# A two-layer sparse-attention and state-space trunk: mask products of four 256-column matmuls, a split PSUM pool, four first tiles side by side, and a bias write in four

## The chip, the cores and the metric

One core of a Trainium2 chip runs the whole program. The metric is the device time of one execution in microseconds (us); lower is better.

## What is computed

The reference is a two-layer trunk on 512 tokens of width 2048, all in float32. Cut to what matters here:

```python
# layer 1: sparse attention, 16 heads of 128; an indexer of 16 small heads picks 128 keys per query
proj = rmsnorm(x) @ w_in                      # q, k, v, gate, index q, index k, index weights
score = einsum('bqsh,bqh->bqs', relu(iq . ik), iw);  idx = top_k(score, 128)
logits = q . k[idx] * scale + rel_bias[rel_bucket(t - idx)]
x = x + (softmax(logits) @ v[idx] * silu(g)) @ w_out
# layer 2: Mamba-2 scan, 64 heads of 64 in 8 groups, chunks of 128 tokens
cb = einsum('bclgn,bcsgn->bgcls', c_, b_)
y_diag = einsum('bgcls,bgrcls,bcsgrp->bclgrp', cb, exp(segsum(a)), x_)   # the masked part
y_off  = einsum('bclgn,bcgrpn,bgrcl->bclgrp', c_, prev_states, exp(a_cs))
x = x + rmsnorm((y_diag + y_off + d_skip * xs) * silu(z), norm_w) @ w_out
```

## The kernel before

**Precision by halves.** A float32 operand is split into a high and a low half, both of a type that TensorE takes in one pass: ScalarE casts the high half (`wh`, `xh`, ...), VectorE subtracts to get the low half (`wl`, `xl`, ...). A product is then three matmuls: high by high, high by low, low by high.

**The dense stream.** Nearly all of TensorE's work is a list of weight tiles (`tiles`), cut into `units` of four blocks of 128 rows. A unit is four steps (a step is a call of `mm`: three matmuls of up to 512 columns into one PSUM bank `acc`). Unit `j` is split into halves while unit `j-3` multiplies (`LEAD`). Each 1 MB tile (`raw`) is loaded by SyncE (SP) when the buffer of the tile three before it is free. The first five tiles are special: for them a unit is four blocks of one tile, and the units go round the five tiles, with loads of 256 KB (`rawu`), first by SP and then by ScalarE's queue.

**The threads.** Everything else (indexer, attention heads, convolution, scan, norms) is written as Python generators that emit instructions between the steps; `yield n` means "go on n steps later". So TensorE's order is fixed when the program is built: small matmuls stand between dense ones, and if an operand is late, TensorE stands still, since it runs in order. The same holds for each other engine.

**The parts that the change touches.**
- `bias_setup` writes a table of relative biases to DRAM (`bias_scr`, 3 MB) by one transfer on SP's queue, during the indexer.
- `index_thread` computes the scores `dots`; `head_thread` computes one attention head: scores `sps`, probabilities in `la`, `lb`, `lc`, their transposes `ptp` in the order of key blocks 0, 1, then 2 and 3, and the products `av` and `av3`.
- `cb_thread` computes C·B for a group, in eight groups: `cpa` holds two products of 256 columns; `cpb` two of 128 columns (blocks 1 and 3), and the transposes of B.
- `m_make` and `m_mul` work for each of 32 pairs of heads: `m_make` builds the masked decay matrices of the blocks 0, 2 (256 columns each) and of the small blocks 1 and 3 together, splits them into `mh` and `ml`, and `m_mul` multiplies them by the scaled inputs `xdhl`, into `y0`, `y1` (256 columns a matmul) and `yc`.
- All PSUM tiles rotate through one pool, `banks`, of eight banks.

Of the kernel before, what the change touches and what calls it, by code (L numbers as in the profile page):

```python
# [42 lines left out]
def kernel(  # L43
# [23 lines left out]
    banks = ctx.enter_context(tc.tile_pool(name="banks", bufs=8, space=bass.MemoryType.PSUM))  # L67
# [9 lines left out]
    def PS(name):  # L77
        return banks.tile([P, S], F32, tag="s", name=name)

# [40 lines left out]
    def cols_load():  # L120
        sy.dma_start(out=cols, in_=cols_in)
        ve.tensor_scalar(out=cols[:, C_CW:C_D], in0=cols[:, C_CW:C_D], scalar1=0.5, scalar2=None, op0=ALU.mult)
# [51 lines left out]
    class Dense:  # L174
        def __init__(self, src, ncol, nk, operand, evac, t0=0, t1=S, packed=False, early=None,
                     order=None, keep=(), given=None):
# [14 lines left out]

        def load_unit(self, u, eng):
            r = T("rawu")
            eng.dma_start(out=r, in_=self.src[:, 4 * u : 4 * u + 4].rearrange("p k j -> p (k j)"))
            self.raw[u] = r
# [18 lines left out]
        def mm(self, u, kk):  # L214
            first = u == self.order[0] and kk == 0
            if first:
                self.acc = PS("acc")
# [19 lines left out]
    class TokenMajor:  # L237
# [21 lines left out]
        def mm(self, u, b):  # L259
            if u == 0 and b == 0:  # L260
                self.acc = [PS("acc") for _ in range(NB)]
# [8 lines left out]
            if u == 15:  # L270
                run(self.evac(out, b))

# [60 lines left out]
    def load_x(k, eng):  # L333
        xf[k] = T("x")
        eng.dma_start(out=xf[k], in_=xT[k])
# [20 lines left out]
    def bias_setup():  # L356
# [10 lines left out]
        sy.dma_start(out=dst, in_=rs[:HA, None, :384].to_broadcast([HA, P, 384]))  # L367
# [38 lines left out]
    def index_thread(iw):  # L406
# [9 lines left out]
        for i in range(1, NB):  # L416
# [91 lines left out]
    def head_thread(h):  # L508
# [43 lines left out]
        for grp in ((0,), (1,), (2, 3)):  # L552
# [182 lines left out]
    def evac_bc(g, which):  # L735
        def go(ps):
# [6 lines left out]
            if which is chl:  # L743
                spawn(cb_thread(g), 11)
        return go

    def cb_thread(g):
        bh, bl, bv = bhl.pop(g)
        ch, cl, _ = chl.pop(g)
        cba, cbb = T("cba"), T("cbb")  # L750
        pa, pb = PS("cpa"), PS("cpb")
        for s, pp in ((0, pa[:, :256]), (2, pa[:, 256:]), (1, pb[:, :P]), (3, pb[:, P:256])):
# [7 lines left out]
        for s in range(2):  # L760
            te.transpose(pb[:, 256 + s * P : 256 + (s + 1) * P], bv[:, s * P : (s + 1) * P], ident)
# [5 lines left out]
        yield 1  # L767
        ve.tensor_tensor(out=cut(cbb)[:, :2], in0=cut(pb)[:, :2], in1=tri2, op=ALU.mult)
        bth, btl = T("bth", F32R)[:, :256], T("btl", F32R)[:, :256]
        yield from split(bth, btl, pb[:, 256:])  # L770
# [45 lines left out]
    def xdt_make(p, d2):  # L816
# [14 lines left out]
        highs, lows = (slice(0, 4, 3), slice(0, 2)), (slice(1, 3), slice(2, 4))  # L831
        for c in range(2):
            sc.copy(out=parts[c][:, :, highs[c]], in_=heads2(v)[:, c:4:2])
        yield HOP
        for c in range(2):
            sub(parts[c][:, :, lows[c]], heads2(v)[:, c:4:2], f(parts[c][:, :, highs[c]]))
        xdt[p] = st

    def pairs_thread(p):
# [6 lines left out]
        yield 8  # L846
# [26 lines left out]
    def m_make(p, m):  # L873
# [19 lines left out]
        hi, lo = T("mh", F32R), T("ml", F32R)  # L893
        yield 1
        yield from split(hi, lo, t)
# [8 lines left out]
    def m_mul(p, m, hi, lo):  # L904
        m_next[0] = (p, m + 1) if m < 2 else (p + 1, 0)
        m_tiles.setdefault(p, []).append((hi, lo))
        if m == 2:
            tiles_m = m_tiles.pop(p)
            ys, yc = [PS("y0"), PS("y1")], PS("yc")
            stat = lambda s, n: xdt[p][s % 2][:, 256 * (s // 2) + P * n : 256 * (s // 2) + P * (n + 1)]  # L910
            two = lambda a: a.rearrange("p (e l) -> p e l", e=2)
            for s, (hi, lo) in zip((0, 2), tiles_m):
                for e in range(2):
                    x = stat(s, e)
                    out = ys[e][:, 128 * s : 128 * s + 256]
                    te.matmul(out, x, hi[:, 256 * e : 256 * e + 256], start=s == 0, stop=False, skip_group_check=True)  # L916
                    te.matmul(out, x, lo[:, 256 * e : 256 * e + 256], start=False, stop=True, skip_group_check=True)  # L917

            hi, lo = tiles_m[2]
            for i, s in enumerate((1, 3)):  # L920
                ls, out = slice(i * P, (i + 1) * P), two(yc[:, 256 * i : 256 * i + 256])
# [11 lines left out]
            odd = lambda a: a.rearrange("p (c h l) -> p c h l", h=2, l=P)  # L933
            for e in range(2):
                r, q = slice(64 * e, 64 * e + 64), slice(64 - 64 * e, 128 - 64 * e)
                ve.scalar_tensor_tensor(out=v[r], in0=x[r], scalar=col(C_D, p)[r], in1=ys[e][r],
                                        op0=ALU.mult, op1=ALU.add)
                yield 1
                add(v[r], v[r], ys[e][q])
                yield 1  # L940
                add(odd(v[r])[:, :, 1], odd(v[r])[:, :, 1], odd(yc[r])[:, :, e])
# [59 lines left out]
    def evac_ob(j):  # L1001
        def go(ps):
            t = PS("x2p") if j >= KD - 5 else T("x2")
# [57 lines left out]
    EARLY_TILES = 5  # L1061
    for t in range(8):
        dense(wa[t], P, 16, opA, evac_iq(t), t0=P, early=t if t < EARLY_TILES else None)
        if t == EARLY_TILES - 1:
            for u in range(4):
                for d in tiles:
                    units.append((d, u))
# [3 lines left out]
    for h in range(HA):  # L1071
# [5 lines left out]
        dense(wa[24 + 2 * h], P, 16, opA, evac_q(h))  # L1077
        dense(wa[25 + 2 * h], P, 16, opA, evac_k(h))
# [28 lines left out]
    at_unit(40, lambda: spawn(bias_setup(), 0))  # L1107
# [175 lines left out]
```

## Time and profile before

| what | value |
|---|---|
| time, median of 3 runs | 2418.91 us (2417.77 to 2419.24) |
| the profiled execution, its own time | 2418.09 us |
| its span, first to last instruction | 2416.4 us |
| TensorE matmuls busy | 2399.8 us, 99% of the span |
| VectorE busy | 1582.5 us, 65% |
| ScalarE busy | 1072.4 us, 44% |
| mean granted TensorE clock | 0.999 of full speed |

The busy time of an engine is the time in which at least one of its instructions was running. Matmuls overlap, so the cost of one in a stream is read from start to start, not from its duration. "Idle before" in brackets is the time for which the engine stood still, with the instruction that ended it.

### The profile page before, as it was taken

What the parts mean: (1) busy time and instruction counts of PE and PEld (TensorE: products, weight loads), DVE (VectorE), ACT (ScalarE), POOL (GpSimd) and SP (SyncE); (2) the same over time, 40 slices, a digit from 0 to 9 for tenths busy, and PEclk for the clock granted to TensorE, in tenths of its full rate; (3) what the DMA queues carried; (4) which work ended last, traced back from release to release, by engine and by line L of the source; (5) the groups of instructions that cost most, each with busy time, mean ns of one, the idle gap of its engine ahead of it and who ended that gap; (6) DMA issues with size and microseconds to landing.
All of it is one profiled execution on the core that took longest, in us unless ns stands there. A gap on an engine that the chain in (4) does not pass through costs nothing.

```text
span 2416.4 us, 29873 instructions
## 1 busy us (share of the span) xinstructions
PE 2399.8 (99%) x11398; PEld 2016.2 (83%) x11398; DVE 1582.5 (65%) x2891; ACT 1072.4 (44%) x2134; POOL 1.2 (0%) x8
## 2 busy tenths in 40 slices
PE   9999999999999999999999999999999999999998
PEld 9878888888888888888888888888888888888887
DVE  6569466464654654358788888888888888433334
ACT  6433233333333433234556565565656566322222
POOL 0000000000000000000000000000000000000000
PEclk9999999999999999999999999999999999999999
DMA  6362322222222224433333333333334344333333
GB/s 223 103 130 88 107 93 74 92 90 90 94 79 93 82 105 142 146 122 130 122 108 119 118 122 126 127 127 106 124 107 142 112 149 157 127 114 100 101 113 109
DMA packets 83440, 278.54 MB, mean 115 GB/s; under 512 B 7744, under 2 KB 40928, under 8 KB 58208
## 3 DMA queue, kind: packets, MB, share of 16 engines
q1 hardware_dynamic: 78976, 266.41, 33.0%
q10 hardware_dynamic: 4320, 10.23, 1.2%
q8 instruction: 89, 1.46, 0.3%
q14 instruction: 55, 0.45, 0.1%
HBM read 258.32 MB, written 18.02 MB: 114 GB/s over the span
## 4 chain that ended last, share of the span: by engine, by line
PE 96%; DVE 2%; DMA 2%; issue 0%; ACT 0%; SPq 0%; DVEq 0%; ACTq 0%
PE acc L229 27%; PE acc L231 27%; PE acc L230 27%; PE acc L265 2%; PE acc L267 2%; PE acc L266 2%; DMA raw<-wa 2%; PE ptp L558 1%; PE y L917 1%; PE y L916 1%; PE xst L819 1%; PE sps L525 0%; PE sps L526 0%; PE sps L524 0%; PE av L588 0%; PE av L586 0%
## 5 line engine op out<-in xcount | busy, mean ns | idle before, releaser
L90 DVE TENSOR_TENSOR wl<-raw,wh 128x512 fp32r<-128x512 f32 (+1 forms) x788 | 528.7, 684 | 136.8 <-ACT wh L206 96.2
L206 ACT CAST wh<-raw 128x512 fp32r<-128x512 f32 (+1 forms) x724 | 427.0, 613 | 173.9 <-PE acc L230 100.1
L229 PE MATMUL acc<-x1h,wh 128*128 128x512 f32 x1280 | 503.4, 393 | 0.0
L230 PE MATMUL acc<-x1l,wh 128*128 128x512 f32 x1280 | 499.5, 390 | 0.0
L231 PE MATMUL acc<-x1h,wl 128*128 128x512 f32 x1280 | 499.2, 390 | 0.0
L229 PE MATMUL acc<-xh,wh 128*128 128x512 f32 (+2 forms) x912 | 353.5, 388 | 2.3 <-ACT wh L206 2.1
L231 PE MATMUL acc<-xh,wl 128*128 128x512 f32 (+2 forms) x912 | 349.6, 383 | 0.3
L230 PE MATMUL acc<-xl,wh 128*128 128x512 f32 (+2 forms) x912 | 348.8, 382 | 0.6 <-DVE xl L101 0.6
L231 PEld LDWEIGHTS acc<-x1h,wl 128*128 128x128 f32 x1280 | 240.4, 188 | 50.9
L229 PEld LDWEIGHTS acc<-x1h,wh 128*128 128x128 f32 x1280 | 240.8, 188 | 46.6
L230 PEld LDWEIGHTS acc<-x1l,wh 128*128 128x128 f32 x1280 | 240.9, 188 | 46.1
L229 PE MATMUL acc<-ygh,wh 128*128 128x512 f32 (+1 forms) x544 | 205.4, 378 | 0.0
L231 PE MATMUL acc<-ygh,wl 128*128 128x512 f32 (+1 forms) x544 | 205.0, 377 | 0.0
L230 PE MATMUL acc<-ygl,wh 128*128 128x512 f32 (+1 forms) x544 | 205.0, 377 | 0.0
L231 PEld LDWEIGHTS acc<-xh,wl 128*128 128x128 f32 (+1 forms) x912 | 170.6, 187 | 35.1 <-DVE wl L90 2.2
L229 PEld LDWEIGHTS acc<-xh,wh 128*128 128x128 f32 (+1 forms) x912 | 170.7, 187 | 31.8 <-ACT wh L206 2.6
L230 PEld LDWEIGHTS acc<-xl,wh 128*128 128x128 f32 (+1 forms) x912 | 171.0, 187 | 29.8 <-DVE xl L101 1.4
L231 PEld LDWEIGHTS acc<-ygh,wl 128*128 128x128 f32 x544 | 102.4, 188 | 18.8
L230 PEld LDWEIGHTS acc<-ygl,wh 128*128 128x128 f32 x544 | 102.4, 188 | 18.7
L229 PEld LDWEIGHTS acc<-ygh,wh 128*128 128x128 f32 x544 | 102.4, 188 | 18.5
L727 DVE SCALAR_TENSOR_TENSOR hh<-rw,cols,hh 128x511 f32<-128x511 f32 x144 | 107.4, 746 | 6.5 <-ACT hh L724 4.0
L887 ACT ACTIVATE bc<-bc,aloc 128x256 f32<-128x256 f32 (+1 forms) x256 | 102.8, 446 | 0.5
(295 smaller groups left out, 3316.1 us busy)
## 6 DMA issues: line engine op xcount, KB each, us to landing
raw<-wb SPq DMA_DIRECT2D x80, 1024.0 KB, 4.9
raw<-wa SPq DMA_DIRECT2D x48, 1024.0 KB, 4.9
raw<-wbo SPq DMA_DIRECT2D x33, 1024.0 KB, 4.8
bc<-r_scr SPq DMA_DIRECT2D x96, 256.0 KB, 6.1
raw<-wav SPq DMA_DIRECT2D x16, 1024.0 KB, 4.9
raw<-wao SPq DMA_DIRECT2D x16, 1024.0 KB, 5.4
yg_scr<-yy SPq DMA_DIRECT2D x24, 256.0 KB, 4.6
ygr<-yg_scr SPq DMA_DIRECT2D x24, 256.0 KB, 5.1
```

What stands on the lines that cost most here:

```text
L90: ve.tensor_tensor(out=out, in0=a, in1=b, op=ALU.subtract)
L206: sc.copy(out=self.w[u][0], in_=self.raw[u].rearrange("p (k j) -> p k j", k=4))
L229: te.matmul(out[:m], w[0], xh[:, ts], start=first, stop=False)
L230: te.matmul(out[:m], w[0], xl[:, ts], start=False, stop=False)
L231: te.matmul(out[:m], w[1], xh[:, ts], start=False, stop=last)
L265: te.matmul(out, xh[:, bs], wh, start=u == 0, stop=False)
L266: te.matmul(out, xh[:, bs], wl, start=False, stop=False)
L267: te.matmul(out, xl[:, bs], wh, start=False, stop=u == 15)
L558: te.transpose(ps[:, n + (i - j) * P : n + (i - j + 1) * P], prob[i][:, j * P : (j + 1) * P], ident)
L727: ve.scalar_tensor_tensor(out=hh[:, d:], in0=rw[:, : S - d], scalar=col(C_CW, 4 * ct + 3 - d), in1=hh[:, d:], op0=ALU.mult, op1=ALU.add)
L819: te.transpose(ps[:, c * P : (c + 1) * P], xs[p][:, c * P : (c + 1) * P], ident)
L887: sc.activation(out=t3[:, e, a:b], in_=t3[:, e, a:b], func=AF.Relu, scale=-1.0, bias=aloc[:, s, 2 * p + e : 2 * p + e + 1])
```

## The change

It does seven things. (1) The small mask blocks 1 and 3 are laid out differently: for each head of the pair and each chunk the high half and the low half of the matrix stand side by side in 256 columns (`m0`, `m1`), so that four matmuls take the place of six, and they add into the same banks as the large blocks; `y` is now two tiles of two banks each, and VectorE adds the parts. (2) Likewise in `cb_thread`: `cc` holds the halves of C side by side, four matmuls take the place of six, VectorE and ScalarE add the two parts (`cbl`), and the transposes of B go into a bank of their own (`bt`), some steps later. (3) The pool of eight banks becomes one of four and, until shortly before layer 2, a second of four (`banks_a`), which then gives way to two pairs of banks (`banks_b`). (4) The first four tiles run side by side: a unit is one block of rows for four tiles, and all their loads are SP's. (5) The bias table is written in four transfers, 24 steps apart. (6) The transposes `ptp` go in the order 2 and 3, then 1, then 0. (7) The state matmuls `st` are two steps later, and a few starting points shift.

```diff
-    banks = ctx.enter_context(tc.tile_pool(name="banks", bufs=8, space=bass.MemoryType.PSUM))
+    banks = ctx.enter_context(tc.tile_pool(name="banks", bufs=4, space=bass.MemoryType.PSUM))
...
+    early_banks.append(early_banks[0].enter_context(
+        tc.tile_pool(name="banks_a", bufs=4, space=bass.MemoryType.PSUM)))
+    def change_banks():
+        early_banks[0].close()
+        late_banks.append(ctx.enter_context(tc.tile_pool(name="banks_b", bufs=2, space=bass.MemoryType.PSUM)))
...
+    class FourTiles:
...
+        def load(self, k):
+            load_x(k)
+            if k < 4:
+                self.raw[k] = T("rawu").rearrange("p (t j) -> p t j", t=4)
+                sy.dma_start(out=self.raw[k], in_=self.src[:4, :, k].rearrange("t p j -> p t j"))
+            elif k % 4 == 0:
+                r = raw_pool.tile([P, 16 * P], F32, tag="raw", name="raw").rearrange("p (t k j) -> p t k j", t=4, k=4)
+                sy.dma_start(out=r, in_=self.src[:4, :, k : k + 4].rearrange("t p k j -> p t k j"))
...
+        def mm(self, k, t):
+            if k == 0 and t == 0:
+                self.acc = [PSA("acc4")[:, : S - self.t0] for _ in range(4)]
+            wh, wl = [a[:, t * P : (t + 1) * P] for a in self.w[k]]
+            xh, xl = [a[:, self.t0 :] for a in xhl[k]]
+            te.matmul(self.acc[t], wh, xh, start=k == 0, stop=False)
+            te.matmul(self.acc[t], wh, xl, start=False, stop=False)
+            te.matmul(self.acc[t], wl, xh, start=False, stop=k == KD - 1)
...
-        sy.dma_start(out=dst, in_=rs[:HA, None, :384].to_broadcast([HA, P, 384]))
+        for g in range(4):
+            hs = slice(4 * g, 4 * g + 4)
+            sy.dma_start(out=dst[hs], in_=rs[hs, None, :384].to_broadcast([4, P, 384]))
+            yield 24
...
-                ps = PS("dots")
+                ps = PS("dots") if h % 3 == 2 else PSA("dots")
...
-        for grp in ((0,), (1,), (2, 3)):
+        for grp in ((2, 3), (1,), (0,)):
...
+            if s % 2:
+                c2 = cc[:, 256 * (s // 2) : 256 * (s // 2) + 256]
+                te.matmul(pp, bh[:, ss], c2, start=s == 1, stop=False, skip_group_check=True)
+                te.matmul(pp[:, :P], bl[:, ss], c2[:, :P], start=False, stop=s == 3, skip_group_check=True)
+                continue
...
+        sc.copy(out=cut(cbl)[:, :2], in_=cut(pb)[:, 1:4:2])
+        yield 2
+        add(cut(cbl)[:, :2], cut(cbl)[:, :2], cut(pb)[:, 0:4:2])
+        ve.tensor_tensor(out=cut(cbb)[:, :2], in0=cut(cbl)[:, :2], in1=tri2, op=ALU.mult)
+        yield 2
+        pt = PS("bt")
+        for s in range(2):
+            te.transpose(pt[:, s * P : (s + 1) * P], bv[:, s * P : (s + 1) * P], ident)
...
-        yield 8
+        yield 10
         st = PS("st")[:, :256]
...
+            hi, lo = T("m0", F32R), T("m1", F32R)
+            cut = lambda a: a.rearrange("p (c x l) -> p c x l", c=2, x=2)
+            src = t.rearrange("p (e c l) -> p e c l", e=2, c=2)
+            for e, a in enumerate((hi, lo)):
+                sc.copy(out=cut(a)[:, :, 0], in_=src[:, e])
+            yield HOP
+            for e, a in enumerate((hi, lo)):
+                sub(cut(a)[:, :, 1], src[:, e], f(cut(a)[:, :, 0]))
...
-                te.matmul(out, stat(s, 0), two(hi)[:, :, ls], start=i == 0, stop=False, skip_group_check=True)
-                te.matmul(out, stat(s, 0), two(lo)[:, :, ls], start=False, stop=False, skip_group_check=True)
-                te.matmul(out, stat(s, 1), two(hi)[:, :, ls], start=False, stop=i == 1, skip_group_check=True)
+            for c in range(2):
+                for e in range(2):
+                    te.matmul(ys[e][:, c, P : 3 * P], stat(2 * c + 1, e), tiles_m[2][e][:, 256 * c : 256 * c + 256],
+                              start=False, stop=True, skip_group_check=True)
...
+    first = FourTiles(wa, [evac_iq(t) for t in range(4)], P)
+    for k in range(KD):
+        units.append((first, k))
+    for t in range(4, 8):
+        dense(wa[t], P, 16, opA, evac_iq(t), t0=P)
...
+        bank = (lambda: PSA("acca")) if h % 4 in (1, 2) else None
+        dense(wa[24 + 2 * h], P, 16, opA, evac_q(h), bank=bank)
+        dense(wa[25 + 2 * h], P, 16, opA, evac_k(h), bank=bank)
...
+    at_unit(u_b - 16, change_banks)
```

Where this moves instructions, first on TensorE, at the end of the mask products of the first pair of heads; before, the last two products of the large blocks are followed by six for the small blocks, into a tile of their own:

```order
L916 MATMUL y1_9855<-mh_9709,xdhl_9566 128x256
L917 MATMUL y1_9855<-ml_9710,xdhl_9566 128x256
L922 MATMUL yc_9856<-mh_9780,xdhl_9567 128x256
L923 MATMUL yc_9856<-ml_9781,xdhl_9567 128x256
L924 MATMUL yc_9856<-mh_9780,xdhl_9567 128x256
L922 MATMUL yc_9856<-mh_9780,xdhl_9567 128x256
L923 MATMUL yc_9856<-ml_9781,xdhl_9567 128x256
L924 MATMUL yc_9856<-mh_9780,xdhl_9567 128x256
L229 MATMUL acc_9794<-x1h_8593,wh_9762 128x512
```

and now by four of the same width, into the tiles of the large blocks:

```order
L1011 MATMUL y_9848<-mh_9703,xdhl_9557 128x256
L1011 MATMUL y_9848<-ml_9704,xdhl_9557 128x256
L1015 MATMUL y_9847<-m0_9781,xdhl_9558 128x256
L1015 MATMUL y_9848<-m1_9782,xdhl_9558 128x256
L1015 MATMUL y_9847<-m0_9781,xdhl_9558 128x256
L1015 MATMUL y_9848<-m1_9782,xdhl_9558 128x256
L244 MATMUL acc_9786<-x1h_8575,wh_9745 128x512
```

The eight products of the large blocks stay; two of 14 matmuls go, for each of 32 pairs. Second, on TensorE in the C·B products of the first group; before, six of 128 columns and then the two transposes of B, between dense matmuls:

```order
L231 MATMUL acc_9330<-x1h_8203,wl_9282 128x512
L755 MATMUL cpb_9363<-bch_9276,bch_9182 128x128
L756 MATMUL cpb_9363<-bcl_9277,bch_9182 128x128
L757 MATMUL cpb_9363<-bch_9276,bcl_9183 128x128
L755 MATMUL cpb_9363<-bch_9276,bch_9182 128x128
L756 MATMUL cpb_9363<-bcl_9277,bch_9182 128x128
L757 MATMUL cpb_9363<-bch_9276,bcl_9183 128x128
L761 MATMUL cpb_9363<-ident_95,bcv_9136 128x128 x2
L229 MATMUL acc_9330<-x1h_8281,wh_9281 128x512
```

and now:

```order
L246 MATMUL acc_9319<-x1h_8419,wl_9290 128x512
L828 MATMUL cpb_9369<-cc_9281,bch_9168 128x256
L829 MATMUL cpb_9369<-cc_9281,bcl_9169 128x128
L828 MATMUL cpb_9369<-cc_9281,bch_9168 128x256
L829 MATMUL cpb_9369<-cc_9281,bcl_9169 128x128
L244 MATMUL acc_9319<-x1h_8497,wh_9289 128x512
```

Six became four, two of them wider; the two transposes stand 18 dense matmuls later, in their own bank. Third, on SP's queue during the indexer, where `bias_scr<-rs` is the bias table's write and `raw<-wa` are weight tiles (in brackets what each waits for: a place among the outstanding transfers, and VectorE's last read of the buffer); before:

```order
L187 DMA raw<-wa 128x2048 [waits DMAHW3_49,DVE_49]
L367 DMA bias_scr<-rs 2048x1x384 [waits DVE_49]
L187 DMA raw<-wa 128x2048 [waits DMAHW4_49,DVE_49]
L187 DMA raw<-wa 128x2048 [waits DMAHW5_49,DVE_49]
L187 DMA raw<-wa 128x2048 [waits DMAHW6_49,DMAHW2_49,DVE_49]
```

and now:

```order
L432 DMA bias_scr<-rs 512x1x384 [waits DVE_49]
L207 DMA raw<-wa 128x2048 [waits DMAHW7_49,DVE_49]
L207 DMA raw<-wa 128x2048 [waits DMAHW0_49,DVE_49]
L432 DMA bias_scr<-rs 512x1x384 [waits DMAHW1_49]
L207 DMA raw<-wa 128x2048 [waits DMAHW3_49,DMAHW2_49,DVE_49]
L432 DMA bias_scr<-rs 512x1x384
L207 DMA raw<-wa 128x2048 [waits DMAHW7_49,DMAHW4_49,DVE_49]
```

The one write of 3 MB ahead of three loads became pieces of a quarter with weight loads between them; a fourth piece follows two loads later.

## Rows read from the trace of the kernel before

**Rows 1.** Page, part 1: busy us (share of the span) xinstructions.

```profile
PE 2399.8 (99%) x11398; PEld 2016.2 (83%) x11398; DVE 1582.5 (65%) x2891; ACT 1072.4 (44%) x2134; POOL 1.2 (0%) x8
```

**Rows 2.** Waits of PE: engine line <- releaser: us in total, times, longest.

```profile
PE acc L229 <- ACT wh L206: 2.1, 2, 1.7
PE st L852 <- DVE xd2l L90: 1.1, 1, 1.1
PE ptp L558 <- DVE lb L548: 1.1, 1, 1.1
...
PE acc L230 <- DVE xl L101: 0.6, 2, 0.3
```

**Rows 3.** Timeline of PE in one pair's mask products: start us, us, instruction.

```profile
1158.99 0.28 PE L916 MATMUL y<-mh,xdhl 128*128 128x256 f32 x1
...
1159.94 0.28 PE L922 MATMUL yc<-mh,xdhl 128*128 128x256 f32 x1
...
1160.66 0.40 PE L229 MATMUL acc<-x1h,wh 128*128 128x512 f32 x1
```

**Rows 4.** Timeline of PE in the first group's narrow C·B products.

```profile
1107.25 0.22 PE L755 MATMUL cpb<-bch 128*128 128x128 f32 x1
...
1107.86 0.41 PE L761 MATMUL cpb<-ident,bcv 128*128 128x128 f32 x2
```

**Rows 5.** Timeline of PE at a 256-column matmul followed by one of 128.

```profile
374.44 0.28 PE L580 MATMUL av<-pth,vh 128*128 128x256 f32 x1
374.55 0.22 PE L581 MATMUL av<-pth,vl 128*128 128x128 f32 x1
374.61 0.45 PE L229 MATMUL acc<-xh,wh 128*128 128x512 f32 x1
374.89 0.39 PE L230 MATMUL acc<-xl,wh 128*128 128x512 f32 x1
```

**Rows 6.** Timeline of the start; the last two rows are matmuls 13 and 22.

```profile
1.73 0.43 SPq L194 DMA_DIRECT2D rawu<-wa  x1
...
5.65 0.62 ACT L206 CAST wh<-rawu 128x512 fp32r<-128x512 f32 x1 [0.56 <-DMA rawu<-wa]
...
6.32 0.44 PE L229 MATMUL acc<-xh,wh 128*128 128x384 f32 x1 [0.42 <-ACT wh L206]
...
7.05 0.44 PE L231 MATMUL acc<-xh,wl 128*128 128x384 f32 x1
...
10.64 0.34 PE L229 MATMUL acc<-xh,wh 128*128 128x384 f32 x1
...
12.20 0.33 PE L229 MATMUL acc<-xh,wh 128*128 128x384 f32 x1
```

**Rows 7.** Windows: us, busy by engine (x instructions), PEclk, DMA share, GB/s.

```profile
28.00:32.00 4.00, 4.00 (x24) 3.89 (x23) 2.48 (x5) 3.09 (x6) 0.00 (x0) 1.00 1.04 397
116.00:138.00 22.00, 22.00 (x106) 18.41 (x105) 9.78 (x19) 7.65 (x17) 0.00 (x0) 1.00 0.92 100
1360.00:1470.00 110.00, 110.00 (x538) 92.81 (x537) 92.95 (x158) 65.65 (x135) 0.00 (x0) 1.00 0.35 122
```

**Rows 8.** Timeline around the bias write, on SP, ACT and PE.

```profile
113.64 0.66 SPq L367 DMA_DIRECT2D bias_scr<-rs  x1
...
151.41 0.62 ACT L206 CAST wh<-raw 128x512 fp32r<-128x512 f32 x1 [12.23 <-DMA raw<-wa]
...
152.08 0.51 PE L229 MATMUL acc<-xh,wh 128*128 128x512 f32 x1 [1.67 <-ACT wh L206]
```

**Rows 9.** Timeline of PE at the two other waits.

```profile
863.60 0.33 PE L558 MATMUL ptp<-ident,lb 128*128 128x128 f32 x1 [1.06 <-DVE lb L548]
...
1249.95 0.39 PE L852 MATMUL st<-xd2l,bth 128*128 128x256 f32 x1 [1.15 <-DVE xd2l L90]
```

**Rows 10.** Timeline of one attention head, from its last transposes to its product.

```profile
366.61 0.38 PE L558 MATMUL ptp<-ident,la 128*128 128x128 f32 x2
367.03 0.48 ACT L567 CAST pth<-ptp 128x384 fp32r<-128x384 f32 x1 [0.97 <-PE ptp L558]
...
367.88 0.28 DVE L90 TENSOR_TENSOR pth<-ptp,pth 128x128 fp32r<-128x128 f32 x1
...
372.86 0.39 PE L586 MATMUL av<-pth,vh 128*128 128x512 f32 x1
```

**Rows 11.** By tile: op xcount, duration ns min/median/max, first and last start, forms.

```profile
L90 DVE TENSOR_TENSOR btl<-cpb,bth x8: 393/418/421, 1114.5 to 1890.1; 128x256 fp32r<-128x256 f32 x8
...
L90 DVE TENSOR_TENSOR ml<-bc,mh x96: 678/685/695, 1137.8 to 2005.4; 128x512 fp32r<-128x512 f32 x96
```

More of the change, by code (lines that the diff above doesn't have):

```diff
@@ L175, in __init__ @@
         def __init__(self, src, ncol, nk, operand, evac, t0=0, t1=S, packed=False, early=None,
-                     order=None, keep=(), given=None):
+                     order=None, keep=(), given=None, bank=None):
+            self.bank = bank
             self.order = list(order or range(nk // 4))
@@ L216, in mm @@
             if first:
-                self.acc = PS("acc")
+                self.acc = self.bank() if self.bank else PS("acc")
             ts, m = slice(self.t0, self.t1), self.ncol
@@ L260, in mm @@
             if u == 0 and b == 0:
-                self.acc = [PS("acc") for _ in range(NB)]
+                self.acc = [PSA("vacc") for _ in range(NB)]
             wh, wl = self.w[u]
@@ L271, in mm, with __init__, split_hi, split_lo @@
                 run(self.evac(out, b))
+    class FourTiles:
+        given, early, nk = None, True, 64
+        def __init__(self, src, evacs, t0):
+            self.src, self.evacs, self.t0 = src, evacs, t0
+            self.raw, self.w = {}, {}
+        def load(self, k):
[6 more added lines that the diff above has]
+                sy.dma_start(out=r, in_=self.src[:4, :, k : k + 4].rearrange("t p k j -> p t k j"))
+                for i in range(4):
+                    self.raw[k + i] = r[:, :, i]
+        def split_hi(self, k):
+            self.x = prep_x(k)
+            next(self.x)
+            self.w[k] = [T("wh", F32R), T("wl", F32R)]
+            sc.copy(out=self.cut(self.w[k][0]), in_=self.raw[k])
+        def split_lo(self, k):
+            for _ in self.x:
+                pass
+            hi, lo = self.w[k]
+            sub(self.cut(lo), self.raw.pop(k), f(self.cut(hi)))
+        def cut(self, w):
+            return w.rearrange("p (t j) -> p t j", t=4)
+        def mm(self, k, t):
[6 more added lines that the diff above has]
+            te.matmul(self.acc[t], wl, xh, start=False, stop=k == KD - 1)
+            if t == 3:
+                del self.w[k]
+            if k == KD - 1:
+                run(self.evacs[t](self.acc[t]))
     tiles = []
@@ L331, with load_x @@
     xf, xhl = {}, {}
-    def load_x(k, eng):
+    def load_x(k):
         xf[k] = T("x")
-        eng.dma_start(out=xf[k], in_=xT[k])
+        sy.dma_start(out=xf[k], in_=xT[k])
     def prep_x(k):
@@ L743, in go @@
             if which is chl:
+                cc = T("cc", F32R)
+                odd = lambda a: a.rearrange("p (c x l) -> p c x l", c=2, x=2)
+                which[g] = (hi, lo, cc)
+                yield 1
+                yield from split(odd(cc)[:, :, 0], odd(cc)[:, :, 1], odd(v)[:, :, 1])
                 spawn(cb_thread(g), 11)
@@ L892, in m_make @@
         ve.tensor_tensor(out=t3, in0=t3, in1=cb[:, None, :].to_broadcast([P, 2, 256]), op=ALU.mult)
-        hi, lo = T("mh", F32R), T("ml", F32R)
         yield 1
-        yield from split(hi, lo, t)
+        if m < 2:
+            hi, lo = T("mh", F32R), T("ml", F32R)
+            yield from split(hi, lo, t)
+        else:
+            hi, lo = T("m0", F32R), T("m1", F32R)
[6 more added lines that the diff above has]
+                sub(cut(a)[:, :, 1], src[:, e], f(cut(a)[:, :, 0]))
         yield 8
@@ L1059, in mark, with half_of_two @@
         return len(units)
[L1061 to L1067, printed above, removed]
+    both = []
+    def half_of_two():
+        if not both:
+            a = PS2("acc2")
+            both.extend([a[:, 0], a[:, 1]])
+        return both.pop(0)
+    first = FourTiles(wa, [evac_iq(t) for t in range(4)], P)
[3 more added lines that the diff above has]
+        dense(wa[t], P, 16, opA, evac_iq(t), t0=P)
     dense(wai, 80, 16, opA, evac_idx)
@@ L1182, in split_now @@
         d.split_lo(u)
-    x0 = prep_x(0)
-    next(x0)
-    d0, u0 = units[0]
-    d0.split_hi(u0)
-    for _ in x0:
-        pass
-    d0.split_lo(u0)
-    for k in range(1, 4):
-        for _ in prep_x(k):
-            pass
-    for i in range(1, LEAD):
+    for k in range(KD):
+        first.load(k)
+        if k == 11:
+            cols_load()
+    for _ in range(3):
+        load_next()
+    for i in range(LEAD):
         split_now(i)
-    spawn(load_early_thread(), 0)
-    spawn(prep_x_thread(), 3)
-    at_unit(12, cols_load)
+    at_unit(20, scale_cols)
     for i in range(u_end):
```

88 lines of the change are left out of this document (28 added, 60 removed).

## The prediction

> **What bounds the kernel now.** I read the busy times first. TensorE is busy 99% of the span, VectorE 65%, ScalarE 44% [rows 1]: as long as TensorE has its operands, only fewer or cheaper matmuls shorten the program, and work on the other engines is free until something on TensorE waits for it. Next the waits of TensorE, to see how often that is so. Four lines hold what matters: 2.1 us for a weight cast (1.7 of it at one place), and 1.1, 1.1 and 0.6 us at three others [rows 2]. So there are two kinds of gain to look for: matmuls taken out, priced from start to start, and a handful of single waits. The windows then say how much room the other engines have in layer 2, where most of the change lies: VectorE is busy 92.95 of 110 us, ScalarE 65.65 [rows 7].
>
> **1. The mask products.** The 14 matmuls of a pair take from 1158.99 to 1160.66, and the six on `yc` from 1159.94 to 1160.66, 0.72 us, so 0.12 us each [rows 3]. Two of the 14 go, with 32 pairs: 64 x 0.12 = 7.7 us. The other twelve keep their width, so nothing else of this changes on TensorE; I take 7.3 to 7.7 us as bounds, the low one if the first of the new ones, with a new stationary operand each, costs 10 ns more.
>
> On the other engines the pair gets dearer. The one subtraction of 512 columns (0.685 us) becomes two of 256 (0.418 each) [rows 11], 0.15 us more for VectorE, and about as much for ScalarE's cast. With the C·B additions (two more VectorE operations of 256 columns for each group of four pairs, 0.84 us, or 0.21 a pair) it is 0.36 us a pair. The 96 subtractions of 32 pairs lie between 1137.8 and 2005.4 [rows 11], 27 us a pair, so a window of 110 us holds about four pairs, and VectorE would go from 92.95 to about 94.4 of 110 us. That is hidden behind TensorE. The cover would be gone if VectorE had 4 us more work in each pair.
>
> **2. The C·B products.** The six narrow ones take from 1107.25 to 1107.86, 0.61 us [rows 4], 0.10 each though they have half the columns of those at 0.12. So the number of matmuls counts here, and hardly the width. A pair of 256 and then 128 columns is seen elsewhere: it starts at 374.44, the dense matmul after it at 374.61, and the one after that at 374.89, where a dense step costs 0.23; the pair thus costs 374.89 - 374.44 - 0.23 = 0.22 us [rows 5]. Two pairs cost 0.44, a saving of 0.17 us a group, 1.3 us over eight groups. Bounds: 1.0 (0.12 for each of the four) to 2.0 (0.18 a pair, if the small delay behind it is not paid twice). The transposes are only moved.
>
> [...]
>
> **3. The start.** The first real matmul starts at 6.32 and the 13th at 10.64; nine more take until 12.20, 0.173 us each [rows 6]. Twelve at that pace are 2.08 us, so 4.32 - 2.08 = 2.24 us are lost while x blocks land one by one, since the first unit needs four of them. With four tiles side by side, the first unit needs one x block and one weight block. What stays is the wait of the third matmul for the first low half: it starts 0.73 us after the first instead of 0.35, 0.38 us. So up to 1.9 us are to be won. Against it: the first weight block comes in 512-byte pieces, one for each tile and partition, instead of 2 KB ones, and TensorE starts when it is cast (issued at 1.73, cast at 5.65, first matmul at 6.32 [rows 6]). 256 KB at the 397 GB/s of the early window take 0.66 us. How much slower the short pieces are, the trace does not show for loads; the nearest it has is the mix with 1 KB pieces in layer 2, 122 GB/s at a share of 0.35, 349 at a full share, against 397/1.04 = 382 [rows 7]. I take half the speed as an estimate, 0.7 us later, and a gain of 1.2 us. Bounds: 1.9 (no loss), and -3 (a quarter of the speed: 2 us more for each of the first four blocks, of which the x blocks and the split hide about half). After the first four blocks the need is 0.5 MB in 2.08 us, 252 GB/s, against 382: no wait.
>
> [...]
>
> **4. The bias table.** Its write is issued at 113.64, and the DMA engines are then 0.92 busy at only 100 GB/s [rows 7, 8]. A weight tile issued behind it lands so late that ScalarE waits 12.23 us for it, and TensorE 1.67 us for the cast [rows 8]. The 3.1 MB at 100 GB/s are 31 us, and a load that shares the engines with all of that came 1.67 us too late. A quarter takes about 8 us, and the pieces are 24 steps apart, 24 x 3 x 0.23 = 17 us, with weight loads between them, so a load meets one of them at most. The wait should go: 1.7 us, bounds 0 and 2.0 (matmuls right behind a wait are slow too). SP's queue holds nothing urgent besides the weight tiles here.
>
> **5. Two single waits.** `st` moves two steps, six dense matmuls or 1.4 us, later; its wait was 1.15 us [rows 9]: gone, or nearly, 1.1 us (bounds 0.4 and 1.4). What is late next is the state product `yo`, and it moves along with it. The transposes of key blocks 2 and 3 go first now and don't need the last probabilities, written into `lb` just before, which cost 1.06 us [rows 9]; by the time block 0 comes they are there: 1.1 us (bounds 0 and 1.2).
>
> **6. Four banks instead of eight.** A PSUM tile now takes the bank of a tile that was read a short time before. The tightest place in a head is `av`, which follows the last transposes. Their last reader ends at 367.88 + 0.28 = 368.16, and `av` starts at 372.86: 4.7 us of room [rows 10]. The new last group is one of 512 columns; its cast and its subtraction together are about 0.3 us longer, which leaves 4.4. And `av` needs the low half from the same subtraction anyway. Layer 2 has fewer tiles in a given time, and its `y` tiles come back after a whole pair. I take 0, bounds 0 and 3 us: should VectorE run late, a bank wait can cost a few single microseconds, as in rows 2.
>
> **The sum.** 7.7 + 1.3 + 1.2 + 1.7 + 1.1 + 1.1 = 14.1 us. The profiled execution took 2418.09 us, of which its span is 2416.4; 2418.09 - 14.1 = 2404.0. The median of the runs is 0.8 us above the profiled one, so against it the same sum gives 2404.8; I say 2404.3, between the two.
>
> **The rivals.**
> - *Only the matmuls count.* Parts 1 and 2 come, 9 us, but the first blocks land late and the waits only move: the short pieces eat the start's gain, and the indexer, whose VectorE work on the top-k also falls here, still waits once. For it: each of the waits is a single event, which a shift of a few steps could bring back elsewhere. Against it: each has a visible cause that the change removes. 2418.1 - 9 + 0 to 4 = 2409 to 2413.
> - *The four banks make each head wait.* If `av` or the next head's `sps` waited in all 16 heads, it would decide from 14.1/16 = 0.88 us a head; at 2 us a head the sum is 2418.1 - 14.1 + 32 = 2436. For it: banks are halved, and in the heads ten tiles rotate through four. Against it: 4.4 us of room at the tightest place, and VectorE has idle time there.
> - *No change.* The first blocks at a quarter of the speed (-3), bank waits (3 us) and the waits that stay (3.9) take 11 us of 14.1: 2415.
> - *Narrow matmuls cost their columns alone.* Then the C·B part gives nothing, 2418.1 - 12.8 = 2405.3. Rows 4 speak against it. [...]
>
> **How the numbers follow.** The forecast, 11 to 17 us gained, has 0.60, and in it the rule on narrow matmuls 0.04. Only the matmuls: 0.29. No change: 0.06. Slower by the banks: 0.05. Its own range is 2401 to 2407.5. The range for 8 in 10 has to take in the larger part of the second case: 2400.8 to 2411. A measurement can tell 0.2%, 4.8 us, from no change. Faster by more: 0.89; within it: 0.06; slower: 0.05.
>
> **What would show it.** Right: 12 matmuls of 0.12 us for a pair; four in C·B in about 0.45 us; the 13th matmul at 9.5 or so instead of 10.64; no wait of ScalarE for a weight tile near 150 us; in the waits of TensorE none for `wh` of 1.7, none on `st` above 0.5, none on `lb`; TensorE's busy time down by about 9 us. Wrong: a wait of `av`, `sps`, `acc` or `dots` for a reader of an earlier tile, repeated in each head or each group; a first matmul after 8 us; VectorE above 97% in layer 2, with TensorE waiting for `wl`; new matmuls slower than 0.13 us where they write into the second half of a bank already in use.

## The result, and the profile after

The changed kernel takes 2440.1 us (median of four runs, 2439.5 to 2441.6), the kernel before 2418.7: a ratio of 1.009, interval 1.0076 to 1.0105. It is slower by 21 us; forecast were 14 us less.

The page of the profile after, part 1 (busy us by engine), beside [rows 1]:

```profile
PE 2396.7 (98%) x11318; PEld 2011.6 (82%) x11318; DVE 1589.6 (65%) x2939; ACT 1075.6 (44%) x2182; POOL 1.2 (0%) x8
```

Its waits of TensorE (us in total, times, longest), beside [rows 2]:

```profile
PE acc L244 <- ACT wh L221: 31.3, 3, 16.7
```

The only other two lines are 1.1 us at the warm-up and 0.3 us at the end. The waits for `xd2l` and `lb` are gone, as forecast. But the wait for a weight cast, 2.1 us before, is now 31.3 us, in three events. Two of the three on TensorE, and the four waits of ScalarE for weight tiles, by the timelines:

```profile
171.07 0.79 PE L244 MATMUL acc<-xh,wh 128*128 128x512 f32 x1 [8.75 <-ACT wh L221]
202.38 0.80 PE L244 MATMUL acc<-xh,wh 128*128 128x512 f32 x1 [16.72 <-ACT wh L221]
...
135.28 0.62 ACT L221 CAST wh<-raw 128x512 fp32r<-128x512 f32 x1 [9.63 <-DMA raw<-wa]
170.40 0.62 ACT L221 CAST wh<-raw 128x512 fp32r<-128x512 f32 x1 [17.29 <-DMA raw<-wa]
201.71 0.62 ACT L221 CAST wh<-raw 128x512 fp32r<-128x512 f32 x1 [20.59 <-DMA raw<-wa]
235.93 0.62 ACT L221 CAST wh<-raw 128x512 fp32r<-128x512 f32 x1 [15.79 <-DMA raw<-wa]
```

All four lie in the stretch of the bias write. SP's queue there, by the timeline:

```profile
99.31 0.79 SPq L432 DMA_DIRECT2D bias_scr<-rs  x1
100.27 13.02 SPq L207 DMA_DIRECT2D raw<-wa  x2
113.33 3.71 SPq L432 DMA_DIRECT2D bias_scr<-rs  x1
124.98 18.47 SPq L207 DMA_DIRECT2D raw<-wa  x1
143.50 3.87 SPq L432 DMA_DIRECT2D bias_scr<-rs  x1
147.47 31.62 SPq L207 DMA_DIRECT2D raw<-wa  x2
179.14 3.72 SPq L432 DMA_DIRECT2D bias_scr<-rs  x1
```

The weight tiles issued between 99.3 and 133 us, by the view of transfers, with their median time from issue to landing at the end:

```profile
raw<-wa SPq DMA_DIRECT2D x3, 1024.0 KB, 35.0
```

One by one, the six tiles issued from 100 to 183 us took 25 to 54 us; elsewhere a tile takes 5. The windows say why (us, busy by engine, granted clock, mean busy share of the 16 DMA engines, GB/s): the first with the first piece under way, the others around the longest wait.

```profile
101.00:108.00 7.00, 7.00 (x35) 5.88 (x34) 3.44 (x8) 2.54 (x6) 0.00 (x0) 1.00 0.23 25
...
195.00:200.00 5.00, 0.00 (x0) 0.00 (x0) 0.00 (x0) 0.00 (x0) 0.00 (x0) 0.50 0.24 57
200.00:205.00 5.00, 2.62 (x6) 2.09 (x7) 2.64 (x5) 3.29 (x8) 0.00 (x0) 0.50 0.25 89
```

The whole write ran at a share of 0.92 and 100 GB/s [rows 7]; a piece runs at 0.23 and 25 GB/s, a quarter of both. 0.79 MB at 25 GB/s are 31 us, as long as the whole took, and it comes four times: by the packet records the four pieces last 29.5 to 31.5 us from first packet to last, the one write before 31.6. While TensorE stands, its granted clock falls to 0.50; it is still there in the first matmuls afterwards, most of which then take 0.43 us from start to start (172 to 174 us) instead of 0.23. From the first `dots` to the first `sps` the program now takes 345.2 - 99.5 = 245.7 us instead of 311.2 - 100.1 = 211.1: 34.6 us lost, of which 31.3 - 1.7 are waits and some 5 the slow matmuls behind them (they cost 7.0 us now, 1.8 before).

The rest of the change looks as forecast. The timeline after: the start (the first weight cast, then TensorE), the first group's narrow C·B products, and the mask products of one pair, beside [rows 3, 4, 6].

```profile
5.11 0.62 ACT L312 CAST wh<-rawu 128x512 fp32r<-128x512 f32 x1 [0.29 <-DMA rawu<-wa]
...
1.12 6.32 PE L126 MATMUL warm<-ones 128*128 128x128 f32 x28 [1.12 <-DVE ones L123]
7.11 0.50 PE L328 MATMUL acc<-xh,wh 128*128 128x384 f32 x1
...
9.36 0.33 PE L328 MATMUL acc<-xh,wh 128*128 128x384 f32 x1
...
1142.05 0.28 PE L828 MATMUL cpb<-cc,bch 128*128 128x256 f32 x1
...
1142.45 0.46 PE L244 MATMUL acc<-x1h,wh 128*128 128x512 f32 x1
...
1191.95 0.28 PE L1011 MATMUL y<-mh,xdhl 128*128 128x256 f32 x1
...
1192.91 0.64 PE L1015 MATMUL y<-m,xdhl 128*128 128x256 f32 x4
1193.39 0.40 PE L244 MATMUL acc<-x1h,wh 128*128 128x512 f32 x1
```

Matmul 13 starts at 9.36 instead of 10.64; the narrow products take 0.40 instead of 0.61 us; a pair takes 1193.39 - 1191.95 = 1.44 us, twelve times 0.12.

### The profile page after: what moved, and what is told of

Same layout as the page of the kernel before. It is cut to its first block, busy times and chain, and to the rows that moved or that the text cites. A ratio compares the mean times of both kernels' runs of the same rounds, so it can differ in the third digit from the quotient of the medians.

```text
span 2439.5 us, 29717 instructions
## 1 busy us (share of the span) xinstructions
PE 2396.7 (98%) x11318; PEld 2011.6 (82%) x11318; DVE 1589.6 (65%) x2939; ACT 1075.6 (44%) x2182; POOL 1.2 (0%) x8
## 3 DMA queue, kind: packets, MB, share of 16 engines
q8 instruction: 88, 1.44, 0.2%
## 4 chain that ended last, share of the span: by engine, by line
PE 94%; DMA 3%; another core or an unknown queue 1%; DVE 1%; ACT 0%; issue 0%; DVEq 0%; ACTq 0%
PE acc L244 23%; PE acc L245 23%; PE acc L246 23%; DMA raw<-wa 3%; PE acca L244 2%; PE vacc L280 2%; PE acca L246 2%; PE vacc L282 2%; PE acca L245 2%; PE vacc L281 2%; PE y L1011 1%; PE ptp L624 1%; PE y L1015 1%; PE xst L902 1%; PE acc L330 0%
## 5 line engine op out<-in xcount | busy, mean ns | idle before, releaser
L107 DVE TENSOR_TENSOR wl<-raw,wh 128x512 fp32r<-128x512 f32 x804 | 539.6, 684 | 187.6 <-ACT wh L221 143.8
L221 ACT CAST wh<-raw 128x512 fp32r<-128x512 f32 x728 | 429.6, 613 | 225.4 <-PE acc L245 99.9
L244 PE MATMUL acc<-xh,wh 128*128 128x512 f32 (+2 forms) x592 | 232.3, 392 | 31.5 <-ACT wh L221 31.3
L246 PE MATMUL acc<-xh,wl 128*128 128x512 f32 (+2 forms) x592 | 229.1, 387 | 0.0
L245 PE MATMUL acc<-xl,wh 128*128 128x512 f32 (+2 forms) x592 | 229.0, 387 | 0.0
L244 PEld LDWEIGHTS acc<-xh,wh 128*128 128x128 f32 (+1 forms) x592 | 111.8, 189 | 52.5 <-ACT wh L221 33.2
L246 PEld LDWEIGHTS acc<-xh,wl 128*128 128x128 f32 (+1 forms) x592 | 111.4, 188 | 23.4 <-DVE wl L107 1.1
L245 PEld LDWEIGHTS acc<-xl,wh 128*128 128x128 f32 (+1 forms) x592 | 111.9, 189 | 19.4
```

What stands on the lines that cost most here:

```text
L107: ve.tensor_tensor(out=out, in0=a, in1=b, op=ALU.subtract)
L221: sc.copy(out=self.w[u][0], in_=self.raw[u].rearrange("p (k j) -> p k j", k=4))
L244: te.matmul(out[:m], w[0], xh[:, ts], start=first, stop=False)
L245: te.matmul(out[:m], w[0], xl[:, ts], start=False, stop=False)
L246: te.matmul(out[:m], w[1], xh[:, ts], start=False, stop=last)
```

## The experiments

The theory: the pieces of the bias write make the loss, since a transfer from few heads runs on few DMA engines. The rivals: another part does (four banks, the loads of the four tiles); four writes on the queue cost by their number; a tile is late only because it stands behind a piece in the same queue.

**One write again**, the rest as changed.

```diff
-        for g in range(4):
-            hs = slice(4 * g, 4 * g + 4)
-            sy.dma_start(out=dst[hs], in_=rs[hs, None, :384].to_broadcast([4, P, 384]))
-            yield 24
+        sy.dma_start(out=dst, in_=rs[:HA, None, :384].to_broadcast([HA, P, 384]))
```

> The changed kernel with the bias table written by one transfer again. Theory (the four pieces of the bias write make the loss, each taking as long as the whole because four heads use a quarter of the DMA engines): the loss of 34.6 us between the indexer and the first head goes but for the 1.7 us that ScalarE's late weight tile cost before; with 0.6 us from the start, 1.1 us before the last head's transposes and 9.7 us in layer 2, as read in the trace of the change, 2418.7 - 11.4 = 2407.3 us (2405 to 2409). Rival (the waits for weight tiles come from another part: four tiles side by side, whose loads all go by SP's queue, or four banks): the three long waits of TensorE stay and it is above 2430 us.

Measured: 2404.8 us (2403.9 to 2405.2), ratio 0.9941 (0.9929 to 0.9954). The loss of 35.3 us is all this part's. It came out 2.5 us below the working, just under its range, since the working had taken only 0.6 us for the start (below, it is worth 2.2). Its waits of TensorE keep one for a weight cast:

```profile
PE acc L244 <- ACT wh L221: 1.0, 1, 1.0
```

**Only this part in the kernel before**: the same edit the other way round.

> The kernel before with only the bias write in four pieces of four heads, 24 steps apart. Theory: all of the loss shows without any other part of the change: 2418.7 + 34.6 - 1.7 = about 2451 us (2444 to 2456). Rival (the pieces only hurt together with the four first tiles or with four banks): within 3 us of 2418.7.

Measured: 2453.5 us (2453.0 to 2454.6), ratio 1.0143 (1.0130 to 1.0157), 34.8 us slower. No other part is needed. Its line in the waits of TensorE:

```profile
PE acc L229 <- ACT wh L206: 29.2, 3, 16.6
```

**Four pieces by rows of the table**, each with all 16 heads.

```diff
-            hs = slice(4 * g, 4 * g + 4)
-            sy.dma_start(out=dst[hs], in_=rs[hs, None, :384].to_broadcast([4, P, 384]))
+            ps = slice(32 * g, 32 * g + 32)
+            sy.dma_start(out=dst[:, ps], in_=rs[:HA, None, :384].to_broadcast([HA, 32, 384]))
```

> The changed kernel with the bias table still written in four pieces, 24 steps apart, but cut by rows of the table: each piece has 32 of the 128 rows of all 16 heads. Theory (the number of heads in a piece sets how many DMA engines work on it): each piece runs at a share of about 0.92 and 100 GB/s and is done in about 8.4 us, no weight tile lands more than about 12 us after its issue, and the 1.7 us of the one write go too: 2404 to 2407 us. Rival (four writes between the weight loads on one queue cost by their number, or a piece of 768 KB is slow however it is cut): weight tiles still land 30 us or more after their issue, and it is above 2425 us.

Measured: 2402.7 us (2402.6 to 2404.1), ratio 0.9935 (0.9922 to 0.9947). **This version is faster than both kernels.** It lies 1.3 us under the range given, which was built on the same working. So it is not the number of writes nor their size. The view of transfers from 95 to 215 us has the median landing times of weight tiles and pieces:

```profile
raw<-wa SPq DMA_DIRECT2D x8, 1024.0 KB, 5.2
bias_scr<-rs SPq DMA_DIRECT2D x4, 768.0 KB, 9.9
```

All waits of TensorE in it, with none for a weight cast:

```profile
PE warm L126 <- DVE ones L123: 1.1, 1, 1.1
PE bc L1131 <- DVE r L377: 0.3, 1, 0.3
```

**Two pieces of eight heads.**

```diff
-        for g in range(4):
-            hs = slice(4 * g, 4 * g + 4)
-            sy.dma_start(out=dst[hs], in_=rs[hs, None, :384].to_broadcast([4, P, 384]))
+        for g in range(2):
+            hs = slice(8 * g, 8 * g + 8)
+            sy.dma_start(out=dst[hs], in_=rs[hs, None, :384].to_broadcast([8, P, 384]))
```

> The changed kernel with the bias table in two pieces of eight heads, 24 steps apart. Theory (engines by the number of heads): each piece runs at a share of about 0.46 and 50 GB/s and takes about 33 us again, so the engines are held for 66 us instead of 134, and the loss lies between that of one write and of four; with (34.6 - 1.7)/3 = 11 us for each piece after the first, 2407.3 + 11 = about 2418 us (2410 to 2424). Rival (time by bytes): a half takes 17 us at 100 GB/s, and it is at 2405 to 2409 us.

Measured: 2414.3 us (2413.5 to 2415.6), ratio 0.9982 (0.9973 to 0.9991), between one write and four. TensorE's waits hold one line for a weight cast:

```profile
PE acc L244 <- ACT wh L221: 8.5, 2, 8.3
```

The window from 101 to 108 us, of two halves and behind it of one write (the last two columns are share and GB/s), shows the steps: a share of 0.23 with four heads (above), 0.46 with eight, 0.92 with sixteen.

```profile
101.00:108.00 7.00, 7.00 (x35) 5.84 (x35) 3.44 (x8) 2.67 (x6) 0.00 (x0) 1.00 0.46 50
```

```profile
101.00:108.00 7.00, 7.00 (x35) 5.88 (x34) 3.44 (x7) 2.17 (x5) 0.00 (x0) 1.00 0.92 100
```

A share of 0.23 could be four engines at work or sixteen that are slowed. The packets in the trace decide it: in this window the view of transfers counts 114, 230 and 454 of them, which by the shares is 0.23 us of an engine's time for each in all three, and no more than 4, 8 and 16 are ever under way at once. So a piece has fewer engines, and they are not slower.

**The four pieces of heads on ScalarE's queue**: in their line `sc.dma_start` takes the place of `sy.dma_start`.

```diff
-            sy.dma_start(out=dst[hs], in_=rs[hs, None, :384].to_broadcast([4, P, 384]))
+            sc.dma_start(out=dst[hs], in_=rs[hs, None, :384].to_broadcast([4, P, 384]))
```

> The changed kernel with its four pieces of four heads each, but issued on ScalarE's queue, while the weight tiles stay on SP's. First theory (a weight tile is late because a quarter of it stands behind the piece in the same queue on the same four engines): from another queue the tiles pass the pieces and land within about 10 us, TensorE's long waits go, and it is at 2403 to 2408 us. Second theory (the four engines are simply taken, whoever issues): a tile still lands about 35 us after its issue, and it stays near 2440 us. [...]

Measured: 2445.0 us (2444.6 to 2445.1), ratio 1.0107 (1.0092 to 1.0123). The time is near the second theory's, but for a reason that neither named. The landing of the weight tiles, by the view of transfers from 95 to 240 us:

```profile
raw<-wa SPq DMA_DIRECT2D x8, 1024.0 KB, 16.8
```

ScalarE's timeline, with its issues of the third and fourth piece and the operation for which it stood still after the fourth:

```profile
134.18 14.25 ACTq L432 DMA_DIRECT2D bias_scr<-rs  x1
...
160.65 18.98 ACTq L432 DMA_DIRECT2D bias_scr<-rs  x1
...
179.68 0.49 ACT L494 ACTIVATE relu<-dots 128x384 f32<-128x384 f32 x1 [16.51 <-issue]
```

Tiles land after 17 us instead of 35, so those from another queue do pass the pieces, though at a third of their usual pace, and ScalarE now waits for none of them. But ScalarE itself is held for 14 and 19 us in the issue of a piece while the earlier ones are still under way, with all its casts behind it: some 10 us of TensorE's waits come then. The larger part, 24.5 us, comes later and has another cause. VectorE stands still until the last piece has landed, presumably because `score` takes the buffer of `rs`, which the write reads. TensorE's waits and VectorE's timeline:

```profile
PE acc L246 <- DVE wl L107: 26.6, 3, 24.5
...
225.94 0.48 DVE L497 TENSOR_SCALAR score<-relu,iwc 128x512 f32<-128x512 f32 x1 [31.18 <-DMA bias_scr<-rs]
```

So a slow write is paid by whoever waits for it: the tiles behind it, the engine that issues it, or the next user of its source. What the tiles' 17 us alone would cost stays open.

**The other parts, undone one at a time in the version by rows.** First the mask products: `m_make`, `m_mul` and `xdt_make` as before the change (six narrow matmuls, `yc` in a `y` tile).

```diff
...
-            for c in range(2):
-                for e in range(2):
-                    te.matmul(ys[e][:, c, P : 3 * P], stat(2 * c + 1, e), tiles_m[2][e][:, 256 * c : 256 * c + 256],
-                              start=False, stop=True, skip_group_check=True)
+            hi, lo = tiles_m[2]
+            for i, s in enumerate((1, 3)):
...
+                te.matmul(out, stat(s, 1), two(hi)[:, :, ls], start=False, stop=i == 1, skip_group_check=True)
...
```

> The version with the bias table cut by rows, with the mask products of the kernel before: 14 matmuls for a pair, six of them for the small blocks. Theory (a matmul of 256 columns costs 0.12 us): 64 more of them, 2402.7 + 7.7 = 2410.4 us (2409.4 to 2411). Rival (the additional subtractions of VectorE, 0.36 us a pair, are not all hidden and take some of the gain): less than 2409.

Measured: 2410.5 us (2410.2 to 2410.5), 7.8 more. The kernel before, measured beside each group of runs, gave 2418.5 to 2418.7 us, so runs of different groups can be set against each other to about 0.2 us.

The C·B products: `cb_thread` as before the change, twice.

```diff
-            if s % 2:
-                c2 = cc[:, 256 * (s // 2) : 256 * (s // 2) + 256]
-                te.matmul(pp, bh[:, ss], c2, start=s == 1, stop=False, skip_group_check=True)
-                te.matmul(pp[:, :P], bl[:, ss], c2[:, :P], start=False, stop=s == 3, skip_group_check=True)
-                continue
...
```

> The version with the bias table cut by rows, with the C.B products of the kernel before: six narrow matmuls for a group instead of four. Theory (the number of matmuls counts): 1.3 us more, 2404.0 us (1.0 to 2.0 more). Rival (narrow matmuls cost their columns alone): no difference, 2402.7 us.

Measured: 2403.2 us (2402.7 to 2403.5), 0.5 more, between the two. So it was run again beside the version itself:

> The version with the bias table cut by rows once more, on the chip of the next three, so that differences of about a microsecond can be read: 2402.7 us, as in its first run, within 0.7.

> The version with the C.B products of before once more, beside the version with the new ones. The traces of the first two runs put the narrow products and the transposes of a group at 0.863 us with the old code and at 0.470 + 0.222 us with the new: 0.17 us for each of eight groups, 1.4 us more in all; the first medians were 0.5 apart. Theory (the trace's difference is real, the first medians scatter): 0.9 to 1.9 us more. Rival (what the rows gain is given back elsewhere): 0.2 to 0.8 us.

Measured: 2402.8 us (2402.5 to 2403.4) and 2403.3 (2403.2 to 2403.5): 0.5 again, the rival's answer. The single times of the two overlap, but the spans of the executions, from first to last instruction, do not: 2400.5 to 2400.9 with the new code, 2401.3 to 2401.6 with the old. TensorE's timeline of the first group, the narrow products and what follows them with the old code, then the transposes `bt` with the new one:

```profile
1101.11 0.22 PE L821 MATMUL cpb<-bch 128*128 128x128 f32 x1
...
1101.89 0.48 PE L244 MATMUL acc<-x1h,wh 128*128 128x512 f32 x1
1102.21 0.39 PE L245 MATMUL acc<-x1l,wh 128*128 128x512 f32 x1
```

```profile
1107.95 0.38 PE L850 MATMUL bt<-ident,bcv 128*128 128x128 f32 x2
1108.08 0.48 PE L244 MATMUL acc<-x1h,wh 128*128 128x512 f32 x1
1108.40 0.40 PE L245 MATMUL acc<-x1l,wh 128*128 128x512 f32 x1
1108.63 0.40 PE L246 MATMUL acc<-x1h,wl 128*128 128x512 f32 x1
1109.05 0.50 PE L244 MATMUL acc<-x1h,wh 128*128 128x512 f32 x1
```

And from the new code's waits between 1103 and 1112 us:

```profile
PEld acc L244 <- ACT cba L841: 0.5, 1, 0.5
```

The delay of the dense matmul behind small ones (0.32 instead of 0.23 us) was paid once a group; with the transposes by themselves it is paid again behind them. And in this first group the next dense tile starts 0.42 us after the matmul before it, since its weight load waits for ScalarE to read `cpa`: a bank wait.

Where the difference builds up is read from the mask products of the first pair of heads and of the last, with the new code, then with the old:

```profile
1153.23 0.28 PE L1011 MATMUL y<-mh,xdhl 128*128 128x256 f32 x1
...
1994.60 0.28 PE L1011 MATMUL y<-mh,xdhl 128*128 128x256 f32 x1
```

```profile
1152.86 0.28 PE L994 MATMUL y<-mh,xdhl 128*128 128x256 f32 x1
...
1995.05 0.28 PE L994 MATMUL y<-mh,xdhl 128*128 128x256 f32 x1
```

Between them stand the products of seven groups, over which the new code gains 0.82 us, 0.12 a group. In the first group, with its bank wait, it loses some 0.16: the old code, ahead by 0.21 us at the first `sps` (306.3 against 306.5), is ahead by 0.37 at the first pair. Together the part is worth some 0.66 us in these traces, and as much in the first two.

The start: five tiles by turns, as before the change, with the starting points that belong to it.

```diff
...
-    first = FourTiles(wa, [evac_iq(t) for t in range(4)], P)
-    for k in range(KD):
-        units.append((first, k))
+    EARLY_TILES = 5
+    for t in range(8):
+        dense(wa[t], P, 16, opA, evac_iq(t), t0=P, early=t if t < EARLY_TILES else None,
+              bank=(lambda: PSA("acc4")) if t < 4 else None)
...
```

> The version with the bias table cut by rows, with the start of the kernel before: five tiles by turns, units of four blocks of rows, loads by SP and then by ScalarE's queue. By the term of the prediction it is 1.2 us more, 2403.9 us. By the matmul numbered 97 in the traces (41.9 and 43.2 us with the old start, 40.2 to 40.7 with the new) it is 1.5 to 2.5 us more, 2404.2 to 2405.2. Rival (the short pieces of the new start cost what it saves): 2402.7 us or less.

Measured: 2405.0 us (2404.2 to 2405.9), 2.2 more.

The two single waits: the order of the transposes and the `st` steps as before.

```diff
-        for grp in ((2, 3), (1,), (0,)):
+        for grp in ((0,), (1,), (2, 3)):
...
-        yield 10
+        yield 8
```

> The version with the bias table cut by rows, with the transposes of the probabilities again in the order of key blocks 0, 1, then 2 and 3, and the state matmuls two steps earlier, as before the change. Theory (each shift removed one wait of 1.1 us): both waits show again on TensorE and the time is 2.2 us more than the same version run beside it (0.4 to 2.6). Rival (the waits only move elsewhere, or other shifts of the change remove them by themselves): no difference within 0.4 us.

Measured: 2405.2 us (2404.9 to 2405.8), 2.4 more, and both waits are back:

```profile
PE ptp L624 <- DVE lb L614: 1.2, 1, 1.2
PE st L935 <- DVE xd2l L107: 1.2, 1, 1.2
```

**The kernel before with the pieces by rows**, the same edit as above, alone.

> The kernel before with only the bias write in four pieces by rows. Theory (the pieces keep all DMA engines, so a weight tile waits for one short piece at most): ScalarE's wait of 12.2 us for a weight tile and TensorE's of 1.7 us behind it are gone, 2418.6 - 1.7 = 2416.9 us (2416.5 to 2417.6). Rival (the tiles of the old start are late for another reason): 2418.6 us.

Measured: 2416.3 us (2415.3 to 2417.5), ratio 0.9991 (0.9982 to 1.0000): 2.4 less. It lies 0.2 us under the range. ScalarE still waits 6.4 us for a weight tile, which the theory had at none, but nothing of it reaches TensorE.

## Why the prediction was wrong

It failed at one step of part 4: "A quarter takes about 8 us ... so a load meets one of them at most." That step divided the time of the whole write by four, as if 100 GB/s were the rate of any piece of it. In these runs the rate goes with the number of heads in a transfer: share and GB/s are 0.23 and 25, 0.46 and 50, 0.92 and 100 for four, eight and sixteen. By that rate a quarter takes as long as the whole, 31 us, and the pieces are issued 14 to 36 us apart, so nearly always one is under way and the weight tiles between them meet it. The term, -1.7 us, was +35.3 against one write. The prediction did not weigh that fewer heads in a piece could mean fewer engines, and so had no rival that ends here. That the rival of four banks was put at 2436 us, near the measured 2440, is chance: in the heads no wait for a bank shows.

| part | forecast, us | measured, us | from |
|---|---|---|---|
| 1 mask products | -7.7 | -7.8 | undone: 2410.5 - 2402.7 |
| 2 C·B products | -1.3 | -0.5 (-0.7 in the traces) | undone, twice |
| 3 start | -1.2 | -2.2 | undone: 2405.0 - 2402.8 |
| 4 bias write | -1.7 | +35.3 | 2440.1 - 2404.8 |
| 4 bias write, by rows instead | not foreseen | -2.1 | 2402.7 - 2404.8 |
| 5 two waits | -2.2 | -2.4 | undone: 2405.2 - 2402.8 |
| 6 four banks | 0 | one wait of 0.5 | weight load behind `cpa` |

TensorE's busy time is 10.6 us lower in the version by rows (2389.2 us; forecast: about 9) and only 3.1 in the changed kernel, whose matmuls behind the waits are slow. VectorE is busy 95.2 us in the window from 1360 to 1470 us (forecast: 94.4), with no wait behind it.

Parts 1, 3 and 5 were right in mechanism. In part 3 the size was off: half speed for the short pieces was the author's estimate, and no run shows it. The part gave 2.2 us against 1.2, and 0.3 above the bound of 1.9, which is within the scatter of the runs. The first weight cast starts at 5.11 us in the changed kernel, 5.65 before [rows 6], so the first block was not late. By the packet records of the two traces, from 2 to 7 us, one of 512 bytes takes 27 ns and one of 2048 bytes 84 ns (medians): the short ones run at 0.78 of the speed, not at half.

In part 2 the narrow matmuls did cost by their number: six took 0.61 us, four 0.40, with 768 columns in both. But "the transposes are only moved" was wrong: alone they pay the small delay a second time. From the first narrow matmul to the second dense one behind, less 0.23, the old code takes 0.87 us, the new 0.46 and for `bt` 0.22, which leaves 0.19 a group. Of this 0.12 arrives, 0.8 in seven groups, and the first group takes 0.2 back; where the other 0.07 goes is not shown. In part 6 that one bank wait is all that shows.

Without the bias write the four parts measured give 7.8 + 0.5 + 2.2 + 2.4 = 12.9 us; the forecast sum without its bias term was 12.4. To see whether anything is left over, both sides need the same write: with the pieces by rows, the kernel before takes 2416.3 us and the changed one 2402.8, 13.5 less. The median spans, which scatter less, give 8.0 + 0.6 + 2.3 + 2.6 = 13.5 for the parts and 2414.5 - 2400.8 = 13.7 in all. What is left is 0.2 us, less than the scatter; the four banks, which no run undoes by themselves, have no larger part in it as far as these sums show.

## What to carry to other kernels

Before a transfer is cut, ask what share of the DMA engines its pieces will have, and read it from a trace. Here pieces of four of the 16 heads ran at 0.23 instead of 0.92 and took some 31 us each, as long as the whole; pieces of 32 of the 128 rows, with all 16 heads in each, ran at 0.93 (101 to 108 us) and landed after 9.9. The slow transfers did their harm through what waited for them: in their queue (31.3 us of TensorE's waits), at their issue (some 10 us) or for their source buffer (24.5 us). So add up how long the engines are held, not the bytes. A sum of small gains on TensorE is worth 14 us here, and one wrong rate on a queue that nothing seemed to need took back more than twice that.

## What was unexpected of the hardware

- Of 16 engines the share is 0.23, 0.46 and 0.92 for 4, 8 and 16 heads, so about 0.06 for each head, at 6.2 GB/s each, which is one engine: a packet takes 0.23 us in all three.
- The issue of a piece holds its engine: on SP 3.7 to 3.9 us with earlier pieces under way, on ScalarE 14 and 19 us for the third and the fourth, after 0.6 for the second; the pieces by rows show none of this (0.3 to 0.4 us).
- The 28 warm-up matmuls at the start are not equally long in every execution: they took 4.78 us in the profiled execution of before and 6.32 in that of the change, in which the first real matmul, at 7.11, came right behind them though its weights were cast by 5.73. The window from 4 to 5 us, shown below, holds 11 of TensorE's matmuls in the first and 7 in the second, at a granted clock of 1.00 in both rows, so that column does not tell of it; what sets the pace there stays open. In the new start it costs nothing later: the version by rows, whose first real matmul in one execution starts at 5.98 us, reaches its first `iwt` (a transpose just before the indexer's scores) at 98.4 us, as the changed kernel does.

The windows from 4 to 5 us, before and then after:

```profile
4.00:5.00 1.00, 1.00 (x11) 1.00 (x10) 0.00 (x0) 0.63 (x1) 0.00 (x0) 1.00 0.92 342
```

```profile
4.00:5.00 1.00, 1.00 (x7) 1.00 (x6) 0.14 (x1) 0.72 (x1) 0.00 (x0) 1.00 0.98 224
```
